# A decoder block in split float32: weight chunks brought in by a casting and an accumulating transfer in place of load, cast and subtraction

## The chip, the core and the metric

The kernel runs on one core of a Trainium2 chip. The metric is the device time of one execution in microseconds; the kernel before has a median of 1076.48 us over three runs (1075.39 to 1076.62).

## What is computed

One decoder block for 512 tokens of width 1024, all in float32, with 16 learned tokens ahead. Two branches read the same normed input: a gated delta rule (8 heads of 128, a causal convolution in front, a recurrence over chunks of tokens) and an attention that keeps the 128 keys with the highest index score for each query. The branches are gated and merged, an output product and a norm follow, then an MLP with a squared ReLU and 4096 hidden columns.

```
n = rmsnorm(h); proj = n @ w_in                      # 1024 x 8280 columns, split into q, k, v, z, gates, index parts
y_gdn = gated_delta_rule(silu(conv(q, k, v)), ...) ; y_dsa = sparse_attention(...)
merged = sigmoid(gate_a) * (y_gdn @ w_branch_gdn) + sigmoid(gate_b) * (y_dsa @ w_branch_dsa)
h = h + rmsnorm(merged @ w_out)
u = square(relu(rmsnorm(h) @ w_up)); h = h + rmsnorm(u @ w_down)
```

## The kernel before, in words

Every dense product is done in three passes so that it keeps float32's precision: both operands are split into a high part, rounded to the format `float32r` in which the tensor engine takes one pass, and a low part, the rest. A product is high x high, high x low and low x high; these three are the three matmul lines in each loop (L193 to L195, L502 to L504, L888 to L890, L1009 to L1011, L1101 to L1103).

The weights come in chunks of 128 partitions x 1024 columns, 512 KB, laid out in memory so that a row of 4 KB is contiguous. There are 152 of them and a smaller one of 704 columns (`misc`) at the start: 8 each for keys, values, queries, the delta rule's gate z, gate a, the first branch product `bg` and the second `bd`; 4 index queries; 12 in the attention (4 queries, 8 of gate b) besides 4 queries, 2 keys and 2 values ahead of it; 8 of the output product; 32 of `w_up` and 32 of `w_down`. The helper `wload` (L90) fetches one: SP issues the load into `raw` (two buffers), the scalar engine copies it with rounding into `hi` (L99), the vector engine subtracts `hi` from `raw` into `lo` (L100). `hi` and `lo` share a ring of five buffers of the tag `hl`; the chunks loaded with `spare` (the second half of the output product's and of the last down product's columns, and two chunks of the first `w_up` group) use other buffers for part of it. In most loops a chunk serves 24 products of 512 columns, for keys, values and queries 48 of 264.

The order of each engine's instructions is made at build time by a planner that takes, by priority (mostly program order), what it thinks ready at that moment by its own costs; `tc.issue_after` and `tc.high_priority` bend it in places. An engine then works through its list in order, and an instruction that waits holds up all behind it. A transfer is issued from the list of an engine: SP's list holds the weight loads, the loads of the activations `hT` (L132), of the tables and of the residual `x`, and the stores of the result. POOL's list holds small loads of constants (L83 to L87), squares of the activations (L138), memsets, the decay rows of the delta rule through memory (L267 to L275), the blocks of its matrix L and of the inverse through memory (L362 to L369, L412 to L426), a selection on `E` (L447), selections in the index scores (L774, L862), loads of norm gains (L1023, L1025, L1086) and the last multiplications (L1139).

The stages follow each other: activations and `misc` (to about 20 us), keys, values and queries with their convolutions (to about 210 us), the inverse and the recurrence with z between (to about 325 us), index scores with gates and the first branch (to about 455 us), attention with its dense products between (to about 600 us), second branch and output product (to about 700 us), and the MLP, whose up and down products alternate in four groups.

Of the kernel before, what the change touches and what calls it, by code (L numbers as in the profile page):

```python
# [10 lines left out]
F32 = mybir.dt.float32  # L11
F32R = mybir.dt.float32r
I32 = mybir.dt.int32
AF = mybir.ActivationFunctionType
ALU = mybir.AluOpType
# [4 lines left out]
P = 128  # L20
# [3 lines left out]
L = 512  # L24
T = NM + L
# [13 lines left out]
def hybrid_block(ctx: ExitStack, tc: tile.TileContext, io: dict):  # L39
# [6 lines left out]
    def f(ap):  # L46
        return ap.bitcast(F32)
# [21 lines left out]
    # ---------------------------------------------------------------- constants  # L69
# [19 lines left out]
    # ---------------------------------------------------------------- weights  # L89
    def wload(src, n, name, spare=False):  # L90
        """one chunk of weights, split; spare: in the buffers tb and st"""
        raw = wp.tile([P, 1024], F32, tag="raw", name=f"raw_{name}", bufs=2)
        nc.sync.dma_start(raw[:, :n], src)
        if spare:
            hi = wk.tile([P, 1024], F32R, tag="tb", name=f"hi_{name}", bufs=2)
            lo = cst.tile([P, 1024], F32R, tag="st", name=f"lo_{name}", bufs=2)
        else:
            hi, lo = (wp.tile([P, 1024], F32R, tag="hl", name=f"{x}_{name}", bufs=5) for x in ("hi", "lo"))
        S.copy(hi[:, :n], raw[:, :n])  # L99
        V.tensor_tensor(lo[:, :n], raw[:, :n], f(hi[:, :n]), ALU.subtract)  # L100
        return hi, lo

    def rsqrt(out, a, shape, tag):
        """out = a ** -0.5 (a > 0): Newton steps from a guess by the exponent"""
# [19 lines left out]
    # ---------------------------------------------------------------- normed activations, transposed and split  # L124
# [19 lines left out]
    def token_scales():  # L144
        """1 / rms of the tokens: on partitions (rn) and along the free axis on every partition (rb)"""
# [26 lines left out]
    # ---------------------------------------------------------------- dense products, weights stationary  # L172
    marks, todo = [], []

    def later(keep=0, part=None):
        """what the tensor engine does with earlier convolved columns, behind a part of the latest products"""
# [7 lines left out]
    def proj_a(w, name, moving=None, m=P, full=True):  # L184
        """columns of one weight chunk [P, 8, m] against the tokens: psum parts [(tile, first column, n)]"""
# [14 lines left out]
    # ---------------------------------------------------------------- small columns: index key, beta, decay, index weights  # L200
# [40 lines left out]
    # cumulated log decay in each chunk (the 16 leading tokens, then chunks of 128)  # L241
# [16 lines left out]
    # rows of gc, through memory, on every partition  # L258
# [10 lines left out]
    # decay between the tokens of a chunk: E[p, (h j), f] = exp(-|gc_p - gc_f|)  # L269
# [14 lines left out]
    # ---------------------------------------------------------------- causal convolution and silu  # L284
    silu = []

    def conv(g, c0, parts_of, out, name, wide=False):
        """out = silu(conv) of the tokens from c0"""
# [17 lines left out]
    # ---------------------------------------------------------------- keys of the delta rule  # L306
# [10 lines left out]
    # XL: blocks 0, 1 (and below them) and 2 of the inverse; XL, L1: the blocks of L below the diagonal of 64 and of 32  # L317
# [20 lines left out]
    def products(x):  # L338
        """L[c, s] = beta_c r_c^2 (k_c . k_s) E of 4 heads (i = h * 4 + j); its blocks on the diagonal, by memory, to lanes"""
# [23 lines left out]
        # lane = x * 64 + i * 4 + block  # L363
# [20 lines left out]
    # ---------------------------------------------------------------- (I + L)^-1: 32-blocks, one on each lane  # L384
# [5 lines left out]
    def substitute(nlane, n, lt, x, tmp):  # L390
        """x = (I + L)^-1 of the block of each lane, then its transpose in tmp; in steps"""
# [42 lines left out]
    # ---------------------------------------------------------------- values of the delta rule: r beta v, tokens on partitions  # L434
    vb = slots.tile([P, 32, P], F32, tag="s5", name="vb")
    vbm = cst.tile([NM, NH, P], F32, tag="st", name="vbm", bufs=2)
    for h in range(NH):
# [4 lines left out]
        if h == 1:  # L442
# [3 lines left out]
            # upper triangle (with the diagonal) of E for the scores  # L446
# [14 lines left out]
    # ---------------------------------------------------------------- queries; scores against the keys of the chunk  # L461
# [32 lines left out]
    # ---------------------------------------------------------------- dense products, tokens stationary  # L494
    def rows_part(pt, pairs, lhs, t, cs, first=True, last=True):
        """adds to one psum tile the products of some chunks [P, 2, 512], (number, (hi, lo)), for the columns cs"""
# [9 lines left out]
    def proj_half(src, name, lhs, evac):  # L506
        """512 columns for all tokens, chunk by chunk of the weights"""
# [8 lines left out]
    def proj_rows(src, name, lhs, evac, done, more=lambda t: None, tail=0):  # L516
        """all columns, so that the tiles of tokens are done one after the other: the first half, then the other tile by tile"""
# [14 lines left out]
    # ---------------------------------------------------------------- output gate of the delta rule: norm * silu(z)  # L532
# [4 lines left out]
    def z_products():  # L537
        """in pieces, for the tensor engine between the steps of others"""
# [33 lines left out]
    # ---------------------------------------------------------------- (I + L)^-1: from 32-blocks to 128  # L572
    # 32 -> 64: Y12 = -Y11 (L21^T Y22)
# [24 lines left out]
    # 64 -> 128  # L598
# [17 lines left out]
    # ---------------------------------------------------------------- the recurrence over the chunks  # L616
    def ktok(cols, n, col, h0, name):
        """keys with their decay to the end of the chunk, tokens on partitions, 4 heads"""
# [613 lines left out]
```

## Time and profile before

| | |
|---|---|
| median of three runs | 1076.48 us |
| span of the profiled execution | 1075.6 us |
| tensor engine busy | 1054.0 us, 98% |
| vector engine busy | 682.8 us, 63% |
| scalar engine busy | 461.4 us, 43% |
| POOL busy | 61.6 us, 6% |
| bytes moved by DMA | 96.44 MB, 90 GB/s in the mean |

The profiled execution's own time isn't listed apart from its span; the span lies within the three runs and 0.9 us under their median. The busy share of the tensor engine is that of matmuls that overlap in the pipeline, so it says that there are few gaps and not that each product is as fast as can be. Issuing a transfer isn't counted as busy time. A line number is that of the kernel before.

### The profile page before, as it was taken

The page shows a single profiled execution, that of the slowest core. Times are in us where ns is not written, and L with a number is a line of the kernel's source. Part 1 is how long each engine was busy: PE and PEld are TensorE (multiplying, and loading weights), DVE is VectorE, ACT ScalarE, POOL GpSimd, SP SyncE. Part 2 cuts the span into 40 slices and gives each one's busy share as a digit, 9 for nine tenths or more (in the row PEclk, how much of TensorE's full clock was granted, in tenths as well). Part 3 has the DMA queues.
Part 4 walks back from the last instruction along what each step waited for, and adds up shares of the span by engine and source line. Part 5 has one row for each costly group of instructions (what it writes and reads, how often), then busy time and mean ns, then how long its engine had stood idle before and what let it go on. Part 6 is the DMA issues. An engine that isn't in the chain of part 4 may idle for free.

```text
span 1075.6 us, 15893 instructions
## 1 busy us (share of the span) xinstructions
PE 1054.0 (98%) x6249; PEld 903.8 (84%) x6249; DVE 682.8 (63%) x1502; ACT 461.4 (43%) x854; POOL 61.6 (6%) x85
## 2 busy tenths in 40 slices
PE   6999999999999999999999999999999999999996
PEld 5999999999997678898888888898888888888885
DVE  5797899516689789957867555695442343343346
ACT  5465555444268432235665432473432332232130
POOL 4202302100000000000000000000000000000022
PEclk9999999998999999999999999999999999999999
DMA  5433424210133022232121235332322333333332
GB/s 177 117 102 108 116 82 136 68 41 2 43 101 115 20 79 80 97 99 82 56 59 59 80 90 187 96 95 83 98 88 90 97 98 98 87 90 98 98 98 79
DMA packets 28235, 96.44 MB, mean 90 GB/s; under 512 B 3632, under 2 KB 3968, under 8 KB 28160
## 3 DMA queue, kind: packets, MB, share of 16 engines
q1 hardware_dynamic: 25440, 87.51, 26.1%
q0 software_dynamic: 2720, 7.92, 2.8%
q8 instruction: 49, 0.80, 0.3%
q14 instruction: 26, 0.21, 0.1%
HBM read 90.14 MB, written 5.28 MB: 89 GB/s over the span
## 4 chain that ended last, share of the span: by engine, by line
PE 89%; DVE 6%; DMA 2%; ACT 2%; issue 1%; SPq 0%; DVEq 0%; ACTq 0%
PE up L1102 5%; PE up L1103 5%; PE up L1101 5%; PE d L503 4%; PE d L504 4%; PE d L502 4%; PE pa_dense L889 2%; PE pa_dense L890 2%; PE pa_dense L888 2%; PE pa_bg L194 1%; PE pa_q L195 1%; PE pa_q L193 1%; PE pa_q L194 1%; PE pa_bg L193 1%; PE pa_bg L195 1%; PE bd L1009 1%
## 5 line engine op out<-in xcount | busy, mean ns | idle before, releaser
L1102 PE MATMUL up<-n2l,hi_up 128*128 128x512 f32 (+1 forms) x288 | 106.8, 372 | 0.0
L1101 PE MATMUL up<-n2h,hi_up 128*128 128x512 f32 (+1 forms) x288 | 106.6, 371 | 0.0
L1103 PE MATMUL up<-n2h,lo_up 128*128 128x512 f32 (+1 forms) x288 | 106.6, 371 | 0.0
L100 DVE TENSOR_TENSOR lo_up<-raw_up,hi_up 128x1024 fp32r<-128x1024 f32 x32 | 39.2, 1225 | 71.0 <-PE up L1102 53.0
L100 DVE TENSOR_TENSOR lo_d<-raw_d,hi_d 128x1024 fp32r<-128x1024 f32 x24 | 29.4, 1226 | 78.4 <-PE d L503 56.0
L502 PE MATMUL d<-hi_d,uh 128*128 128x512 f32 x192 | 75.9, 396 | 0.0
L504 PE MATMUL d<-hi_d,ul 128*128 128x512 f32 x192 | 75.9, 395 | 0.0
L503 PE MATMUL d<-lo_d,uh 128*128 128x512 f32 x192 | 75.9, 395 | 0.0
L1102 PEld LDWEIGHTS up<-n2l,hi_up 128*128 128x128 f32 x288 | 54.2, 188 | 10.3
L1101 PEld LDWEIGHTS up<-n2h,hi_up 128*128 128x128 f32 x288 | 54.2, 188 | 10.3
L1103 PEld LDWEIGHTS up<-n2h,lo_up 128*128 128x128 f32 x288 | 54.1, 188 | 10.3
L1105 ACT ACTIVATE rup<-up 128x512 f32<-128x512 f32 (+1 forms) x36 | 19.9, 552 | 99.6 <-PE up L1103 99.6
L99 ACT CAST hi_d<-raw_d 128x1024 fp32r<-128x1024 f32 x24 | 25.2, 1049 | 59.6 <-PE d L504 59.6
L99 ACT CAST hi_up<-raw_up 128x1024 fp32r<-128x1024 f32 x32 | 33.4, 1044 | 24.0 <-PE d L504 22.7
L504 PEld LDWEIGHTS d<-hi_d,ul 128*128 128x128 f32 x192 | 36.1, 188 | 8.7
L502 PEld LDWEIGHTS d<-hi_d,uh 128*128 128x128 f32 x192 | 36.1, 188 | 8.7
L503 PEld LDWEIGHTS d<-lo_d,uh 128*128 128x128 f32 x192 | 36.1, 188 | 8.7
L888 PE MATMUL pa_dense<-nhi,hi_dense 128*128 128x512 f32 x96 | 39.3, 409 | 0.0
L889 PE MATMUL pa_dense<-nlo,hi_dense 128*128 128x512 f32 x96 | 38.0, 396 | 0.0
L890 PE MATMUL pa_dense<-nhi,lo_dense 128*128 128x512 f32 x96 | 38.0, 396 | 0.0
L546 PE MATMUL pb_z<-hi_z,nhi 128*128 128x256 f32 x128 | 37.9, 296 | 0.0
L193 PE MATMUL pa_k<-nhi,hi_k 128*128 128x264 f32 x128 | 37.1, 290 | 0.0
(570 smaller groups left out, 3079.3 us busy)
## 6 DMA issues: line engine op xcount, KB each, us to landing
raw_up<-w_up SPq DMA_DIRECT2D x32, 512.0 KB, 3.6
raw_d<-w_down SPq DMA_DIRECT2D x24, 512.0 KB, 3.6
raw_k<-w_k SPq DMA_DIRECT2D x8, 512.0 KB, 4.1
raw_v<-w_v SPq DMA_DIRECT2D x8, 512.0 KB, 4.2
raw_q<-w_q SPq DMA_DIRECT2D x8, 512.0 KB, 3.5
raw_z<-w_z SPq DMA_DIRECT2D x8, 512.0 KB, 3.6
raw_w_ga<-w_ga SPq DMA_DIRECT2D x8, 512.0 KB, 3.6
raw_bg<-w_bg SPq DMA_DIRECT2D x8, 512.0 KB, 3.6
```

The costliest lines, as they stand in the source:

```text
L99: S.copy(hi[:, :n], raw[:, :n])
L100: V.tensor_tensor(lo[:, :n], raw[:, :n], f(hi[:, :n]), ALU.subtract)
L193: TE.matmul(pt[:m, :n], hi[:, ws], mh[:, k, ms], start=(k == 0), stop=False)
L502: TE.matmul(pt, lh, whi, start=beg, stop=False)
L503: TE.matmul(pt, lh, wlo, start=False, stop=False)
L504: TE.matmul(pt, ll, whi, start=False, stop=end)
L888: TE.matmul(pt, hi[:, ws], nhi[:, k, NM:], start=(k == 0), stop=False)
L889: TE.matmul(pt, hi[:, ws], nlo[:, k, NM:], start=False, stop=False)
L890: mm = TE.matmul(pt, lo[:, ws], nhi[:, k, NM:], start=False, stop=(k == KT - 1))
L1101: TE.matmul(pt, hi[:, ws], n2h[:, k, ms], start=(k == 0), stop=False)
L1102: TE.matmul(pt, hi[:, ws], n2l[:, k, ms], start=False, stop=False)
L1103: TE.matmul(pt, lo[:, ws], n2h[:, k, ms], start=False, stop=(k == KT - 1))
```

## The change

Only `wload` changes; the other differences are removed comments. The load into `raw` goes, and with it the buffers `raw`. POOL issues a transfer from memory straight into `hi`, whose format differs from the source's, so that the transfer casts. The scalar engine then writes -`hi` into `lo`. POOL issues a second transfer of the same chunk from memory into `lo`, which adds to what stands there: `lo` becomes the source less `hi`. The subtraction on the vector engine goes. The ring `hl` has seven buffers in place of five.

```diff
     def wload(src, n, name, spare=False):
-        raw = wp.tile([P, 1024], F32, tag="raw", name=f"raw_{name}", bufs=2)
-        nc.sync.dma_start(raw[:, :n], src)
         if spare:
             hi = wk.tile([P, 1024], F32R, tag="tb", name=f"hi_{name}", bufs=2)
             lo = cst.tile([P, 1024], F32R, tag="st", name=f"lo_{name}", bufs=2)
         else:
-            hi, lo = (wp.tile([P, 1024], F32R, tag="hl", name=f"{x}_{name}", bufs=5) for x in ("hi", "lo"))
-        S.copy(hi[:, :n], raw[:, :n])
-        V.tensor_tensor(lo[:, :n], raw[:, :n], f(hi[:, :n]), ALU.subtract)
+            hi, lo = (wp.tile([P, 1024], F32R, tag="hl", name=f"{x}_{name}", bufs=7) for x in ("hi", "lo"))
+        G.dma_start(hi[:, :n], src)
+        S.activation(lo[:, :n], f(hi[:, :n]), AF.Copy, scale=-1.0)
+        G.dma_start(lo[:, :n], src, accum_op=ALU.add)
         return hi, lo
```

## Rows read from the trace of the kernel before

**Rows 1.** The page's busy time of each engine, with share and instructions.

```profile
PE 1054.0 (98%) x6249; PEld 903.8 (84%) x6249; DVE 682.8 (63%) x1502; ACT 461.4 (43%) x854; POOL 61.6 (6%) x85
```

**Rows 2.** Waits of the tensor engine: us in total, times, longest.

```profile
PE pa_misc L193 <- ACT hi_misc L99: 6.6, 1, 6.6
PE pa_misc L193 <- ACT nhi L135: 2.4, 1, 2.4
PE pa_misc L194 <- DVE nlo L136: 1.0, 1, 1.0
PE vtp L453 <- ACT cy_v L303: 0.9, 1, 0.9
```

**Rows 3.** Timeline of the scalar engine in the MLP: start, duration, instruction, idle before.

```profile
859.53 0.60 ACT L1105 ACTIVATE rup<-up 128x512 f32<-128x512 f32 x1 [3.44 <-PE up L1103]
...
865.15 0.60 ACT L1105 ACTIVATE rup<-up 128x512 f32<-128x512 f32 x1 [3.43 <-PE up L1103]
```

**Rows 4.** The page's costliest groups: a chunk's subtraction and cast; busy, mean ns.

```profile
L100 DVE TENSOR_TENSOR lo_up<-raw_up,hi_up 128x1024 fp32r<-128x1024 f32 x32 | 39.2, 1225 | 71.0 <-PE up L1102 53.0
...
L99 ACT CAST hi_up<-raw_up 128x1024 fp32r<-128x1024 f32 x32 | 33.4, 1044 | 24.0 <-PE d L504 22.7
```

**Rows 5.** Timeline of the scalar engine at the start: a scaled copy.

```profile
4.87 0.73 ACT L135 ACTIVATE nhi<-xr,gT 128x528 fp32r<-128x528 f32 x1 [2.57 <-DMA xr<-hT]
```

**Rows 6.** DMA queues (q1: SP's, q0: POOL's): packets, MB, share of 16 engines.

```profile
q1 hardware_dynamic: 25440, 87.51, 26.1%
q0 software_dynamic: 2720, 7.92, 2.8%
```

**Rows 7.** Timeline of POOL, where its dense stretches begin and end, and its waits.

```profile
2.95 0.53 POOL L87 DMA_DIRECT2D dtb<-dt_bias  x1
...
41.44 0.52 POOL L267 DMA_DIRECT2D gcd<-gts  x1 [15.59 <-DVE gts L264]
...
50.67 0.53 POOL L275 DMA_DIRECT2D zsp<-gcdm  x1
90.22 0.96 POOL L392 MEMSET sub<- 128x1024 f32 x1 [39.02 <-PE kss L333]
...
100.55 1.27 POOL L368 COPY lam<-lhs 32x512 f32<-32x512 f32 x2
...
111.35 1.16 POOL L362 DMA_DIRECT2D ld<-lhs  x1 [8.43 <-DVE lhs L360]
...
119.74 1.89 POOL L368 COPY lam<-lhs 32x512 f32<-32x512 f32 x2
...
175.17 0.53 POOL L425 DMA_DIRECT2D ym__1009<-zsp  x1 [51.61 <-DVE zsp L400]
...
191.09 0.65 POOL L417 DMA_DIRECT2D Yb<-yd  x1
...
385.55 0.29 POOL L774 TENSOR_SCALAR_AFFINE_SELECT mask<-mask 128x128 f32<-128x128 f32 x1 [16.24 <-DVE mask L772]
```

**Rows 8.** Transfers by issuing queue: count, KB each, median us from issue to landing.

```profile
raw_up<-w_up SPq DMA_DIRECT2D x32, 512.0 KB, 3.6
...
ld<-lhs POOLq DMA_DIRECT2D x2, 1024.0 KB, 7.2
...
xd<-sub POOLq DMA_DIRECT2D x1, 512.0 KB, 5.2
```

**Rows 9.** The chain that ended last, in the keys: start, duration, piece.

```profile
57.28 1.11 PE kss L333 x10
64.32 1.11 PE kss L333 x10
```

**Rows 10.** Timeline of the tensor engine at the start.

```profile
7.32 0.42 PE L194 MATMUL pa_misc<-nlo,hi_misc 128*88 128x264 f32 x1
7.54 0.47 PE L195 MATMUL pa_misc<-nhi,lo_misc 128*88 128x264 f32 x1
...
19.81 0.28 PE L193 MATMUL pa_k<-nhi,hi_k 128*128 128x264 f32 x1
```

**Rows 11.** A window of the MLP: busy us by engine, granted clock, DMA share, GB/s.

```profile
800.00:900.00 100.00, 100.00 (x430) 80.45 (x429) 33.19 (x35) 32.22 (x43) 0.00 (x0) 1.00 0.31 95
```

## Prediction

> **What bounds the kernel now.** I read the page's busy shares first, then who waits for whom on the tensor engine, then one chunk of the MLP as a timeline, then the DMA views, and last the timeline of POOL, the queue into which the change moves the weights.
>
> The tensor engine is busy for 98% of the span, the vector engine for 63%, the scalar engine for 43%, POOL for 6% [rows 1]. What the tensor engine waited for is 10 us at the start, for the first weights and activations (6.6, 2.4 and 1.0), and later one wait of 0.9 us [rows 2]; the five left out have 0.2 to 0.8 us each. It never waited for a weight chunk behind the first. In the MLP a chunk of 512 KB gives 24 products of 512 columns; the activation behind one follows the one before after 5.62 us (859.53, 865.15) [rows 3], and the tensor engine fills that time. So the weights need only be in place in time, and they are. An engine that is relieved off this path gives back at most what the tensor engine waits for it: some 3 us.
>
> The span is 1075.6 us; the three runs have a median of 1076.48, so I work from the span and add 0.9.
>
> **What goes.** 152 chunks (and one small one) lose a subtraction on the vector engine, 1.23 us each [rows 4], together 187 us of its 683. Almost all of it lies beside products. Of the stalls that it may have a part in, 0.9 us before a transpose and 1.0 us at the start [rows 2] among them, I count -2 us (bounds 0 and -3). SP loses its 152 loads; it keeps the activations and tables, and nothing waits for SP.
>
> **What stays in size.** The scalar engine's cast of a chunk (1.04 us [rows 4]) becomes a scaled copy of the same 1024 columns. The nearest row for a scaled copy is 0.73 us for 528 columns [rows 5], so at most 1.4 us for 1024; once in 5.62 us that changes nothing.
>
> **What is added: two transfers in series on POOL's queue.** Neither a casting nor an accumulating transfer stands in the trace, so I bound them by plain rows.
>
> First the rate. SP's queue moved 87.51 MB in 26.1% of 16 engines' span [rows 6]: 87.51 / (16 x 0.261 x 1075.6 us) is 19.5 GB/s for each engine, so 512 KB take 1.68 us of all 16. POOL's queue moved 7.92 MB in 2.8%, 16.4 GB/s, or 2.0 us for 512 KB, with smaller packets among them. For the cast I take 1.68 to 2.0 us. The accumulation must read memory and the buffer, twice the reading: 3.4 to 4.0 us if reading sets the pace. The pair then needs 5.0 to 6.0 us of the DMA engines in each 5.62 us. That is the narrowest place of this change: at 5.0 it is hidden, at 6.0 each chunk comes 0.4 us late.
>
> No row shows an accumulation, so here a page speaks. The Trainium skill, "Collectives: The Full Stack", section "The bandwidth ceiling: the fold count and why AG ≠ RS ≠ AR", says that a reduction in the DMA path is slow because it reads two sources, not because it adds, and gives 31 GB/s over two engines for it. By that, as an estimate, 16 engines would take 2.1 us for 512 KB, the pair about 4 us, and the MLP's term below would fall to 0. I keep the rows' own 5.0 to 6.0.
>
> Second the latency. With 7 buffers taken in turn, the low part of chunk i gets the buffer of the high part of chunk i-3, and the high part of chunk i that of the low part of chunk i-4. So the low part may be begun when chunk i-3 ends and is wanted when chunk i-1 ends: two chunks, 11.2 us in the MLP. In it lie the activation that is ahead on the scalar engine and the scaled copy (0.6 [rows 3] and 1.05 to 1.4), the issue on POOL (0.5 to 1.2 us [rows 7]) and the landing. For the landing the nearest rows are 3.6 us for a chunk from SP's queue, 5.2 us for 512 KB from POOL's, and 7.2 us for 1 MB from POOL's, which moves as much as an accumulation reads [rows 8]; I take 6 to 7.2. The chain is 8 to 10 us; with the next high part in front on the same queue (1.7 to 2.0 us) it is 10 to 12. If the chain is 12, three chunks take 12 + 5.62, that is 5.87 for each instead of 5.62.
>
> So rate and latency both sit at the edge, between 0 and 0.4 us for each chunk. Chunks at this pace: 64 of the MLP, 8 of the second branch product, 16 of the first gates and branch, 88 in all. 88 x 0.4 is 35 us at most; I take 0.16 each, **+14 us**, nearer the hidden end, because a plain load of 4 KB rows is the nearer row for both rates.
>
> **What POOL's order adds.** POOL works through its queue in order, so a load stands behind whatever waits there: the low part's accumulation itself waits for the scalar engine, and behind it the next high part, memsets, copies and stores of the delta rule. Before, POOL's waits hurt nobody. Four stretches are dense [rows 7]: 41.4 to 51.2 us (decay rows, eight broadcasts), 90.2 to 101.8 (a store, a read that waits for it, copies), 111.4 to 121.6 (the same and a selection), 175.2 to 191.7 (blocks of the inverse): 9.8, 11.6, 10.2 and 16.6 us. A chunk of the keys lasts 7.0 us [rows 9], so the chain of 8 to 10 us leaves 4 to 6 us of two chunks to spare. If loads stood wholly behind each stretch, the losses beyond 5 us would be 4.8 + 6.6 + 5.2 + 11.6 = 28 us. If the planner sets loads between these instructions, they are near 0. I take a third, **+10 us**. Later POOL waits for the vector engine's index scores four times, for instance 16.2 us before the selection at 385.6 [rows 7]. A load behind it would lose up to 11 us, one ahead of it nothing; these loads are free early, and I take **+2 us**.
>
> **The start.** The first weights now go behind POOL's three small loads, whose last begins at 2.95 us [rows 7]; the first product waited 6.6 us [rows 2], the first with a low part began at 7.54 us [rows 10]. Now: issue at 3.5, landing 3.6 to 7.2 later, copy 0.8, issue 0.7, landing 5.2 to 7.2 again: low part at 14 to 19 us. Before, the stage waited 2.4 and 1.0 us for activations anyway [rows 2], and the next stage's first product came at 19.81 us [rows 10]. 32 of the 48 products need no low part and can run meanwhile; the other 16 begin 0.22 us apart, as 7.32 and 7.54 [rows 10]. Done at 18 to 23 us instead of 19.8; the next chunk's low part queues behind. Bounds -1 and +8, taken **+4 us**.
>
> **Sum.** 1075.6 + 14 + 10 + 2 + 4 - 2 = 1103.6; with the 0.9, **1104.5 us**. The forecast's own range is 1085 to 1130.
>
> **Rivals.**
> *The DMA engines become the bound.* If an accumulation doesn't overlap with its neighbours, or the cast slows its transfer too, the pair exceeds 5.62 us, and from there each further microsecond costs 88. With 6.6 us it is 86 us on top of the other 14 (POOL, the start, less DVE): 1176 us. With 7.2 us, one landing time of 1 MB, it is 139: 1230. For it speaks that POOL's queue was the slower one per byte [rows 6]; against it that plain rows already give 5.0. Chance 0.25, from 1130 to 1230.
>
> *All of it is hidden, not slower.* The DMA pair stays at 5.0 us, the planner sets the loads ahead of POOL's waits, and the start hides behind the activations' own waits (2.4 and 1.0 us [rows 2]). It decides where the chain stays under two chunks everywhere. Then the change is -3 to +2 us: 1073 to 1078.6. Against it: four dense stretches and the series of two landings at the start. Chance 0.16.
>
> *A load behind a long wait on POOL.* POOL waited 51.6 us for the substitution before the store at 175.17, and up to 16.2 us later [rows 7]. If the planner takes that vector work for earlier than it is, loads stand behind it: about 45 us beyond the spare time, on top of the 28: 1150 us. Chance 0.08.
>
> *POOL can't write its transfers while the vector engine works.* In the trace the same pair of copies on POOL took 1.27 us at 100.55 and 1.89 us at 119.74 [rows 7], so POOL is slowed by something there. If each issue grew by 0.7 us, a chain with two would be 1.4 us longer and a chunk 0.47 us: 88 x 0.47 = 41 more, 1146 us. The Trainium skill, "SBUF — State Buffer", section "Who interferes with whom", says that a vector instruction in a two-port mode holds the port pair that POOL needs for descriptors. By that rule it would come so only beside copies and scalar operations, of which the MLP has few. Chance 0.04.
>
> That the transfer doesn't round, both formats having 4 bytes, would leave a low part of zero and the same time: no case of its own.
>
> **How the numbers follow.** Forecast 0.47, then 0.25, 0.16, 0.08, 0.04. A measurement of this kernel can tell about 0.2%, 2.15 us, from no change. Below 1074.3 lies 0.06 (part of the hidden case), between 1074.3 and 1078.6 0.10, above 0.84. The range 1075 to 1200 leaves out about 0.08 below and 0.10 above, the DMA bound at its worst.
>
> **What would show it.** SP's queue should fall from 87.5 MB to about 8, POOL's rise to some 160, and the DMA share in the MLP from 0.31 [rows 11] to about 0.9. The vector engine should lose some 187 us. New waits of the tensor engine should name transfers into low parts: short ones spread over the MLP (rate or latency), and blocks of several microseconds near 45, 95, 115 and 185 us (POOL's order). If the activations of the MLP still follow each other after 5.62 us, the 14 us are wrong; if after 6.5, the DMA bound holds. No wait at all, or waits on the scalar engine's negatives instead of transfers, would make the reasoning wrong.

## The result, and the profile after

The changed kernel takes 1135.22 us in the median (1130.21 to 1143.03, 4 runs) beside 1076.55 for the kernel before: 1.0548 times as long, 95% interval 1.0505 to 1.0591. I had forecast 1104.5, so the side was right and the rise forecast was half of the measured one. Runs of one kernel differ with the granted clock: these four from 1130.21 us at a mean clock of 0.978 to 1143.03 at 0.966, and those of before, over all chips, from 1075.4 to 1092.8. The profiled execution has a span of 1134.9 us, 59.3 more than the 1075.6 of before. Lines of code below are the changed kernel's: L97 the casting transfer, L98 the negative, L99 the accumulating transfer.

The page's busy times (answers [rows 1]), its two DMA queues ([rows 6]), the negative of an up chunk (mean 1061 ns, [rows 4]), the transfers of these chunks with their median landing ([rows 8]), and, in a fence of its own, the window of the MLP ([rows 11]):

```profile
PE 1072.5 (95%) x6249; PEld 918.4 (81%) x6249; DVE 518.4 (46%) x1349; ACT 463.4 (41%) x854; POOL 278.1 (25%) x391
...
q0 software_dynamic: 46784, 168.04, 68.9%
q1 hardware_dynamic: 3408, 7.44, 1.9%
...
L98 ACT ACTIVATE lo_up<-hi_up 128x1024 fp32r<-128x1024 f32 x32 | 34.0, 1061 | 75.2 <-DMA hi_up<-w_up 35.5
...
hi_up<-w_up POOLq DMA_DIRECT2D x32, 512.0 KB, 5.2
lo_up<-w_up POOLq DMA_DIRECT2D x32, 512.0 KB, 7.5
```

```profile
800.00:900.00 100.00, 100.00 (x429) 80.39 (x428) 15.93 (x23) 36.09 (x48) 26.35 (x37) 1.00 0.92 196
```

The change does what it says: the vector engine loses 164 us, the weights have moved to POOL's queue twice over, and in the MLP the DMA engines' share rises from 0.31 to 0.92. And there the tensor engine is busy for all of the 100 us at full clock, as before. POOL's 278.1 us contain its issues, contrary to what is said of issues beside the table of before: the page counts the 32 of the up chunks' high parts as 18.4 us. The time was lost elsewhere. The tensor engine's waits (us in total, times, longest; answers [rows 2]):

```profile
PE pa_misc L192 <- DMA hi_misc<-w_misc: 12.4, 1, 12.4
PE pa_misc L194 <- DMA lo_misc<-w_misc: 7.9, 1, 7.9
PE pa_v L194 <- DMA lo_v<-w_v: 5.7, 2, 4.5
PE is L765 <- DVE iq L745: 4.9, 1, 4.9
PE pb_z L546 <- DMA lo_z<-w_z: 4.9, 2, 3.6
PE kss L332 <- ACT cy_k L325: 3.3, 1, 3.3
PE up L1102 <- DMA lo_up<-w_up: 3.0, 1, 3.0
PE pa_q L194 <- DMA lo_q<-w_q: 2.9, 1, 2.9
PE oa L502 <- DMA lo_oa<-w_out: 2.6, 1, 2.6
PE pa_k L194 <- DMA lo_k<-w_k: 2.3, 1, 2.3
PE bd L1010 <- DMA lo_bd<-w_bd: 2.0, 1, 2.0
```

Eight of the eleven lines name a low part, that is the second transfer of a chunk. All waits of this view come to 53.7 us, those of before to 12.7: 41 of the 59.3. The rest is about what the granted clock costs. The windows of 10 us around the waits of the keys (3.3 and 2.3) show it; the columns are busy us of PE, PEld, DVE, ACT and POOL, the granted clock, the DMA share and GB/s:

```profile
55.00:65.00 10.00, 6.66 (x57) 6.43 (x56) 7.99 (x17) 4.77 (x11) 1.58 (x2) 1.00 0.52 153
65.00:75.00 10.00, 7.56 (x33) 6.95 (x33) 5.29 (x9) 4.43 (x10) 2.50 (x4) 0.50 1.05 222
75.00:85.00 10.00, 10.00 (x84) 9.68 (x83) 3.01 (x4) 5.07 (x10) 1.93 (x3) 0.99 0.74 147
```

From 65 to 75 us the clock is at 0.50, its lower level of 1.2 GHz, and then full again. The stretch begins 1.2 us behind the stall of 3.3 us; the one of 2.3 us lies in it. The record of the granted clock has eight such stretches between the start and the tail, of 3.4 to 10.2 us, 51.0 together; in before it has one (6.8 us, in the recurrence). Six of the eight, 34.0 us, begin in a stall of 2.0 to 4.9 us or at most 1.2 us behind it; 6 us of them lie inside stalls, and half of the other 28 is 14 us. The two others (10.2 us in the recurrence, 6.8 in the index scores) follow no wait and cost 8.5, before's one 3.4. That makes 19 us, beside 18 that the waits leave over.

Where the tensor engine falls behind is read from the first product of each stage, in us later than in before. The other columns are experiments that follow:

| stage begins | after | x4 | x9 | x10 | x17 | x16 | x1 |
|---|---|---|---|---|---|---|---|
| keys | 11.0 | 8.9 | -1.9 | 5.3 | 8.7 | -1.0 | 6.6 |
| values | 19.9 | 16.4 | 0.0 | 3.7 | 14.9 | -0.9 | 4.8 |
| queries | 26.2 | 16.9 | 7.6 | 1.6 | 22.1 | -1.1 | 9.5 |
| z, recurrence | 29.6 | 18.1 | 11.0 | 3.0 | 22.2 | -1.1 | 17.3 |
| index scores | 37.8 | 30.3 | 16.2 | 3.9 | 24.8 | -1.1 | 20.7 |
| attention | 47.5 | 50.8 | 25.8 | 23.0 | 40.1 | -1.1 | 20.8 |
| second branch | 48.4 | 51.3 | 26.7 | 23.6 | 40.6 | -1.3 | 20.4 |
| output product | 52.3 | 52.5 | 28.8 | 23.6 | 40.7 | -1.2 | 20.5 |
| up products | 55.9 | 54.8 | 33.6 | 24.4 | 41.5 | -0.4 | 20.5 |
| down products | 59.3 | 58.7 | 37.2 | 24.1 | 46.0 | 7.4 | 21.8 |
| last product | 59.3 | 58.7 | 37.2 | 24.1 | 46.0 | 7.4 | 21.8 |

After loses 30 us up to z, 8 in z and the recurrence, 10 in the index scores, 12 from the attention to the first chunks of the MLP, and nothing behind them.

Two places show how a stall comes about. At the start (timeline of the tensor engine, answers [rows 10]):

```profile
12.39 0.49 PE L192 MATMUL pa_misc<-nhi,hi_misc 128*88 128x264 f32 x1 [12.39 <-DMA hi_misc<-w_misc]
...
21.47 0.52 PE L194 MATMUL pa_misc<-nhi,lo_misc 128*88 128x264 f32 x1 [7.92 <-DMA lo_misc<-w_misc]
```

The first transfer was issued at 3.52 us beside the eight loads of the activations and landed 8.7 us later; its negative stood behind squares in the scalar engine's list until 15.69; the second transfer was issued at 16.77 and landed at 21.4. In the values, the timelines of the scalar engine and of POOL around the wait of 4.5 us:

```profile
132.73 1.06 ACT L98 ACTIVATE lo_v<-hi_v 128x1024 fp32r<-128x1024 f32 x1 [1.65 <-DMA hi_v<-w_v]
```

```profile
130.90 3.97 POOL L446 TENSOR_SCALAR_AFFINE_SELECT E<-E 128x4096 f32<-128x4096 f32 x1
136.50 1.11 POOL L363 DMA_DIRECT2D lam<-ld  x1 [1.63 <-DMA ld<-lhs]
137.65 1.47 POOL L367 COPY lam<-lhs 32x512 f32<-32x512 f32 x2
139.18 1.04 POOL L368 COPY lam<-lhs 64x1024 f32<-64x1024 f32 x1
140.17 0.94 POOL L99 DMA_DIRECT2D lo_v<-w_v  x1
```

The negative is there at 133.8, but the accumulation is issued only at 140.17, behind a selection, a read that waits for a store, and copies. Something else stands beside the selection: of 24 steps of the vector engine on `cy_v`, 0.76 us in the median, the one begun at 131.21 took 4.2 us.

### The profile page after: what moved, and what is told of

It is laid out like the page before. It is cut to its first block, busy times and chain, and to the rows that moved or that the text cites. A ratio compares the mean times of both kernels' runs of the same rounds, so it can differ in the third digit from the quotient of the medians.

```text
span 1134.9 us, 15954 instructions
## 1 busy us (share of the span) xinstructions
PE 1072.5 (95%) x6249; PEld 918.4 (81%) x6249; DVE 518.4 (46%) x1349; ACT 463.4 (41%) x854; POOL 278.1 (25%) x391
## 3 DMA queue, kind: packets, MB, share of 16 engines
q0 software_dynamic: 46784, 168.04, 68.9%
## 4 chain that ended last, share of the span: by engine, by line
PE 68%; issue 11%; DMA 8%; DVE 8%; ACT 3%; POOL 2%; SPq 0%; DVEq 0%; POOLq 0%; ACTq 0%
PE up L1102 5%; PE up L1101 5%; PE up L1100 5%; PE d L503 4%; PE d L502 4%; PE d L501 4%; PE pa_dense L887 2%; PE pa_dense L888 2%; PE pa_dense L889 2%; DVE cy_v L300 2%; PE pa_w_ga L192 1%; PE pa_w_ga L193 1%; PE pa_w_ga L194 1%; PE pa_bg L192 1%; PE pa_bg L193 1%
## 5 line engine op out<-in xcount | busy, mean ns | idle before, releaser
L1106 DVE TENSOR_TENSOR uup<-rup 128x512 f32<-128x512 f32 (+1 forms) x36 | 22.7, 632 | 144.5 <-ACT rup L1104 144.5
L98 ACT ACTIVATE lo_up<-hi_up 128x1024 fp32r<-128x1024 f32 x32 | 34.0, 1061 | 75.2 <-DMA hi_up<-w_up 35.5
L1100 PEld LDWEIGHTS up<-n2h,hi_up 128*128 128x128 f32 x288 | 54.7, 190 | 10.2
L1101 PEld LDWEIGHTS up<-n2l,hi_up 128*128 128x128 f32 x288 | 54.6, 189 | 10.2
L98 ACT ACTIVATE lo_d<-hi_d 128x1024 fp32r<-128x1024 f32 x24 | 25.4, 1060 | 83.2 <-DMA hi_d<-w_down 57.2
L97 POOL DMA_DIRECT2D hi_up<-w_up x32 | 18.4, 574 | 114.7 <-PE up L1102 62.2
L194 PE MATMUL pa_v<-nhi,lo_v 128*128 128x264 f32 x128 | 37.4, 294 | 5.7 <-DMA lo_v<-w_v 5.7
L546 PE MATMUL pb_z<-lo_z,nhi 128*128 128x256 f32 x128 | 37.6, 294 | 4.9 <-DMA lo_z<-w_z 4.9
L194 PE MATMUL pa_k<-nhi,lo_k 128*128 128x264 f32 x128 | 37.8, 299 | 2.3 <-DMA lo_k<-w_k 2.3
L194 PE MATMUL pa_q<-nhi,lo_q 128*128 128x264 f32 x128 | 36.4, 285 | 2.9 <-DMA lo_q<-w_q 2.9
```

What stands on the lines that cost most here:

```text
L98: S.activation(lo[:, :n], f(hi[:, :n]), AF.Copy, scale=-1.0)
L194: mark = TE.matmul(pt[:m, :n], lo[:, ws], mh[:, k, ms], start=False, stop=(k == KT - 1))
L546: TE.matmul(pt, nhi[:, k, ts], wlo, start=False, stop=False)
L1100: TE.matmul(pt, hi[:, ws], n2h[:, k, ms], start=(k == 0), stop=False)
L1101: TE.matmul(pt, hi[:, ws], n2l[:, k, ms], start=False, stop=False)
L1106: V.tensor_tensor(u, r, r, ALU.mult)
```

## The experiments

Theories at the outset: **Q**, the order: loads stand behind what waits in POOL's list, negatives behind the scalar engine's. **T**, the transfers: two for each chunk, one after the other, each slower than a plain one and colliding with others on the 16 engines. Later **C**: a stall lowers the clock, so it costs more than its length; **C2**: in the index scores the order of the products alone lowers it. Ratios are to the runs of the kernel before on the same chip.

### One part at a time: x1, x2, x3

All three start from the kernel before, with its two raw buffers and its ring of five. x1 (shown): the raw loads from POOL. x2: the high part by the casting transfer from POOL, the low part still by SP's raw load and the subtraction. x3: the low part by negative and accumulation.

```diff
-        nc.sync.dma_start(raw[:, :n], src)
+        nc.gpsimd.dma_start(raw[:, :n], src)
```

> The kernel before, with its plain weight loads issued from POOL's list instead of SP's; cast and subtraction stay. Theory Q (order: the loads stand behind POOL's other work and the scalar engine's): the single transfer needs no second issue, but it waits in the same list, so a good part of the 59 us should appear, 1095 to 1120 us. Theory T (transfers: two in series, and slower ones): one plain transfer per chunk, so nearly no loss, 1076 to 1085 us.

> The high part by the casting transfer from POOL; the low part as before, a plain load by SP and the subtraction on the vector engine; the bytes moved double. Theory Q: the high parts wait in POOL's list, 1090 to 1115 us. Theory T: the casting transfer alone is about a plain one and nothing follows it in series but a subtraction, 1076 to 1090 us.

> The high part as before (plain load by SP, cast on the scalar engine); the low part by the negative and the accumulating transfer from POOL. Theory Q: the accumulation still waits in POOL's list and behind the scalar engine's negative, 1095 to 1120 us. Theory T: the series of two transfers stays, only the first is a faster one (3.6 us to land instead of 5.2), and the start's series too: 1100 to 1125 us. If the accumulation were harmless, under 1085 us.

x1: 1103.39 us, ratio 1.0245 (1.0220 to 1.0271). x2: 1114.96, 1.0356 (1.0302 to 1.0411). x3: 1276.6 (1256 to 1289), without a ratio. x1 and x2 lie in theory Q's ranges, x2 at their upper end, x3 beyond those of both. POOL's queue with two raw buffers thus costs 27 us, nearly what I had forecast for the whole change, with plain transfers and one for each chunk: at the start (6.6) and from the values to the index scores (4.8 to 20.7, table). x2 has two transfers for each chunk, neither behind the other, and loses 38 us, 24.7 of them up to the index scores; its longest wait behind the start, 5.3 us, is for a high part. So a series isn't needed for a loss; the few buffers of x1 and x2 are a cause that no run tries by itself. x3 is worse than the whole change, with waits for low parts all over the MLP:

```profile
PE d L504 <- DMA lo_d<-w_down: 25.7, 14, 2.7
PE up L1104 <- DMA lo_up<-w_up: 15.0, 16, 2.4
```

It keeps the ring of five, in which a low part takes the buffer of the high part two chunks back; with the change's seven it is three chunks back. I take that chunk of time for what lets the MLP of after hide its accumulations; no run varies the ring by itself.

### The transfers by themselves: x5

Twelve chunks of 512 KB for each way, the decoder block left out.

> The disputed cost by itself; the whole block is left out. Five phases, each behind the one before: 12 plain chunk loads from SP, 12 plain from POOL, 12 casting, 12 accumulating, then 6 casting and 6 accumulating in turns, each of 512 KB, back to back. Theory T: the accumulation is the slow one, 3.4 to 4.5 us each against 1.6 to 2.0 for the others, and a pair in turns takes 5 us or more. Theory Q: all four kinds stream alike, under 2.2 us each, a pair under 4.4 us.

The page's row of GB/s, 40 slices of 4.86 us: plain from SP (305 to 417), plain from POOL (356 to 419), casting (343 to 417), accumulating (205 to 213), and pairs of casting and accumulating (224 to 290):

```profile
GB/s 0 0 0 305 409 417 165 0 0 55 356 419 414 69 343 417 414 104 0 0 34 208 205 211 212 208 213 4 0 0 146 224 267 290 284 84 0 0 187 246
```

A row of 4 KB takes a DMA engine 159 ns plain from either queue, 174 casting, 328 accumulating: 1.27, 1.39 and 2.62 us for 512 KB (8 rows on each of the 16 engines). A pair takes 4.0 us by that sum, within the 5.62 us of a chunk in the MLP. Casting is almost free, and the accumulation takes 2.06 times a plain load.

### What the accumulation costs in place: x10, x17

```diff
-        G.dma_start(lo[:, :n], src, accum_op=ALU.add)      (x10: gone)
+        G.dma_start(lo[:, :n], src)                        (x17: overwrites the negative)
```

> The changed kernel without the accumulating transfer: the low part is left at the high part's negative, so the low products are computed with other values. What stays is the casting transfer from POOL, the scalar engine's negative and seven buffers. Theory T: the second transfer carries more than half of the 59 us, 1085 to 1105 us. Theory Q: it is the lists' order, which stays, 1110 to 1130 us.

> After, with the second transfer of each chunk as a plain casting one that overwrites the negative: the low part is then the rounded weights themselves and not the remainder. The order of all instructions, the buffers, the waits and the number of transfers stay; only a row of 4 KB takes 174 ns of a DMA engine instead of 328, as measured alone. If what the accumulation costs is its time on the DMA engines (collisions with tables, activations and the delta rule's transfers): most of the 33 us by which after is behind the kernel without the second transfer comes back: 1100 to 1115. If it is the second transfer in series, begun behind the scalar engine's negative and POOL's list, with its landing of some 4 to 5 us instead of 7.5: 1118 to 1135.

x10: 1101.68, ratio 1.0214 (1.0164 to 1.0265). x17: 1125.56, 1.0420 (1.0350 to 1.0489). The whole change is at 1.0548, so of its 59 us some 23 stay without a second transfer, 22 come with a second transfer of any kind, and 14 with its adding. Without it, POOL's lists and the first transfers cost 3.9 us up to the index scores (table; 1.6 to 5.3 on the way), beside 24.8 in x17 and 37.8 in after. 19 of the 23 fall in the index scores at half clock, which comes and goes between runs (below; x10's four went from 1092 to 1105), so the split is better read ahead of that stage: 4, 21 and 13 us. The tensor engine's waits of x10, and then of x17:

```profile
PE pa_misc L191 <- DMA hi_misc<-w_misc: 12.5, 1, 12.5
PE pa_misc L193 <- ACT lo_misc L98: 2.6, 1, 2.6
PE pk L650 <- ACT osb L667: 1.0, 1, 1.0
```

```profile
PE pa_v L194 <- DMA lo_v<-w_v: 6.2, 2, 3.2
PE pa_misc L194 <- DMA lo_misc<-w_misc: 6.0, 1, 6.0
PE up L1102 <- DMA lo_up<-w_up: 4.2, 1, 4.2
```

Low parts are late in x17 as in after, though each row takes 174 ns and not 328; those of the queries, the second branch and the output product no longer are. So most of the cost is that of a second transfer, whatever it does. I put it down to the series: the second can be issued only when the first has landed and the negative is made. No run has a second transfer outside the series with these buffers, so its traffic isn't told apart from its place.

### Whose list: x4, x8, x9

x4: after, with POOL's 21 other transfers moved to SP. x8: after, the negative on the vector engine. x9: after, with the first four chunks (`misc`, three keys) the old way.

```diff
-        S.activation(lo[:, :n], f(hi[:, :n]), AF.Copy, scale=-1.0)
+        V.tensor_scalar(lo[:, :n], f(hi[:, :n]), -1.0, None, ALU.mult)      (x8)
```

> The changed kernel, with all 21 places of POOL's other transfers (constants, decay rows, blocks of L and of the inverse, gains) issued from SP's list, which the change has emptied; POOL keeps memsets, copies, selections and the weights. Theory Q: the blocks near 45, 130 and 185 us go, 1105 to 1120 us, and the stalls that stay are at the start and where the scalar engine's list is late. Theory T: nothing moves, 1130 to 1140 us, because the same transfers still share the 16 engines.

> After, with the negative made by the vector engine in place of the scalar engine: nothing else changes, both transfers stay. Theory Q in its second form (the accumulation waits for its negative, which stands behind squares, copies and exponentials in the scalar engine's list): the low parts of the first chunks, of the keys and of the values come some microseconds earlier and 1110 to 1125 is to be expected. Theory T (the second transfer itself, begun after the first has landed): the negative only changes its list, the vector engine has long lists of its own in keys, values and index scores, and the time stays at 1128 to 1145.

> The changed kernel, with the first four chunks (misc and three of the keys) brought in the old way: plain load by SP, cast, subtraction. If the start's 11 us come from the series of two transfers, the keys begin at about 20 us and the whole ends 10 to 18 us earlier, 1117 to 1126 us. If later waits only move, the end stays at 1130 to 1137.

x4: 1132.0, ratio 1.0486 (1.0439 to 1.0533). It gains 10 us in the values and queries (table: 16.9 and 18.1 instead of 26.2 and 29.6), so the case at 140.17 us is real, and loses them again in the recurrence and the index scores, where 30.7 us ran at half clock. As a whole it lies in theory T's range, and its interval overlaps after's. x8: 1149.78, 1.0645 (1.0585 to 1.0706), slower than either theory said: its waits for lo_v reach 10.6 and for lo_q 8.6 us. By the index scores it is 7 us behind after (45.0 and 37.8); the rest of the 17 us between the two traces comes in that stage, with 34.1 us at half clock. x9: 1121.26, 1.0430 (1.0384 to 1.0477), in the range expected: the start is gone (-1.9 at the keys), the rest stays.

### What a stall costs: x6, x11

x6 repeats the subtraction of three chunks. x11 makes the fourth chunk of groups 1 to 3 wait for the activation of the third (shortened: `x` is the chunk's high part with `n` 1, 4 and 12, and its low part with 1; the two chunks behind it get one pass for each part):

```diff
+    for _ in range(n):
+        V.scalar_tensor_tensor(x[:, :512], r_of_third_chunk, 0.0, f(x[:, :512]), ALU.mult, ALU.add)
```

> The kernel before with three stalls made on purpose in the MLP, 100 us and more apart: the subtraction of one chunk is repeated, 5, 8 and 12 times in all (4.9, 8.6 and 13.5 us later), of which the chunk's spare time hides some 4.4 us. If a stall costs what it lasts, the stalls of about 0.5, 4 and 9 us make 13.5 us: 1090 us. If each also leaves the tensor engine at the low clock for a stretch, as in the changed kernel's record of the clock (3.4 to 10.2 us at 0.5), each of the two long ones costs 2 to 5 us more: 1094 to 1100 us.

> The kernel before, with the loads as they were. In the up products of groups 1, 2 and 3 the weights of the fourth chunk are made to wait for the activation of the third: 1, 4 and 12 passes of the vector engine (0.69 us each for 512 columns, as the squares in the MLP of before take) add zero times that activation to the high part, one more to the low part (the fifth and sixth chunk get one pass for each part, which fit beside products). So the tensor engine must stand three times: about 0.6 us for the activation, 0 to 0.7 for the square that may stand ahead, and 0.69 for each pass: 1.5 to 2.7 us, 4 to 5, and 9.5 to 10.5, together 15 to 18 us. No transfer is added. If a stall of the tensor engine itself brings the half clock (theory C, the term missing from the sum), the two long stalls, and perhaps the short one, are each followed within some microseconds by a stretch at half of the granted clock of 3.4 to 10 us, which costs half of its length again: 1095 to 1103 us, the mean clock of the MLP under 1. If the low clock of after comes from the transfers' traffic or from something else in its early stages, the clock stays full in the MLP and the time is 1091.5 to 1094.5.

x6: 1080.37, ratio 1.0029 (1.0018 to 1.0041). The delays were hidden; the longest stall was 1.2 us and no half clock followed it, so it told nothing of theory C. x11: 1105.18, ratio 1.0252 (1.0215 to 1.0288). The three stalls came out at 2.38, 6.6 and 12.41 us, 21.4 together, and the kernel takes 28.7 us more in the profiled execution. The windows behind each (granted clock is the third number from the end):

```profile
772.00:775.00 3.00, 2.81 (x8) 2.12 (x9) 2.45 (x5) 0.09 (x1) 0.00 (x0) 0.64 0.56 175
...
870.00:875.00 5.00, 4.61 (x11) 3.68 (x12) 0.25 (x1) 0.00 (x0) 0.00 (x0) 0.50 0.00 0
876.00:881.00 5.00, 5.00 (x23) 4.04 (x22) 2.76 (x4) 2.16 (x3) 0.00 (x0) 1.00 0.16 15
...
967.00:981.00 14.00, 6.02 (x14) 4.79 (x15) 7.56 (x12) 0.00 (x0) 0.00 (x0) 0.51 0.00 0
981.00:990.00 9.00, 9.00 (x40) 7.19 (x39) 4.64 (x6) 2.88 (x5) 0.00 (x0) 1.00 0.22 58
```

In 5 us at half clock 11 products run, and 23 in the next 5 us. The half clock lasted from 772.8 to 776.2, 868.4 to 875.2 and 967.4 to 981.0. Product by product against before, the three places cost 4.2, 9.0 and 15.4 us. Less the stalls that is 1.8, 2.4 and 3.0, half of the part of each stretch that lies behind its stall (3.4, 4.8 and 6.0 us). So a stall alone, with the old loads, brings the half clock here, and theory C holds. It is no rule for every stall: in after those of 2.9 us in the queries and 2.6 in the output product were followed by none. The Trainium skill, "TensorE: Matmul & The Clock Gate", section "Terms", prices throttled time in the same way: time that runs at half of the clock costs half of its length; this trace agrees.

### Where the MLP stands: x12, x16

The new way for the 64 chunks of the MLP alone. In x12 the others came the old way with all their chunks in the ring of seven; in x16 they keep the buffers of before.

> After's way for the 64 chunks of the MLP alone; the other 89 come by SP's plain load, the scalar engine's cast and the vector engine's subtraction, their raw chunks in the same ring of seven. If the MLP hides the pair of transfers (in after nothing was lost there behind its first chunks, at a DMA share of 0.9 and more): 1076 to 1080, and only the four chunks that start the MLP together may cost something (in after 3.0 us of waits and a stretch at half clock, so at most 6 us: 1083), with the granted clock as in before. If the MLP of after was hidden only because something ahead of it was late, or if the DMA bound of my prediction holds: 1085 and above, the up and down products late by 0.1 us and more for each chunk.

> The new way for the 64 chunks of the MLP alone, as before tried, but now the 89 other chunks keep their two raw buffers and the ring of five, and the MLP's chunks go through these seven in turn. So the stages ahead are those of the kernel before, product by product. If the MLP hides the pair of transfers: 1076 to 1082, with at most the 3.6 us that the last trial lost behind the first four chunks of the up product. If the DMA bound of my prediction holds in the MLP (a pair over 5.62 us): 1130 and more; if the pair is at the edge, as my sum had it (0.16 for each of 64 chunks): 1086.

x12: 1113.76, ratio 1.0313 (1.0257 to 1.0370), but 32 us of that are lost ahead of the MLP, where I had also changed the ring for the old loads; how much is the ring's no run shows. x16: 1085.08, 1.0056 (1.0012 to 1.0101). It is level with before up to the MLP, loses all of it at the first four up chunks, which are begun together, and nothing in the 60 behind (table: 7.4 and 7.4). Its waits:

```profile
PE up L1116 <- DMA hi_up<-w_up: 3.7, 1, 3.7
PE up L1118 <- DMA lo_up<-w_up: 2.5, 2, 1.9
```

The two long ones (3.7 and 1.9 us) and half of the 5.5 us at half clock behind them are the whole loss. The time is near the 1086 of the expectation for a pair at the edge, but by accident: that loss would be spread over 64 chunks. The MLP hides the pair wherever the loads are ahead.

### The index scores: x13, x14b, x15

x10 loses 19 us in this stage with no wait over 1 us in it. Its windows:

```profile
370.00:380.00 10.00, 10.00 (x22) 5.29 (x22) 7.01 (x19) 4.26 (x10) 0.28 (x1) 0.63 0.20 53
380.00:390.00 10.00, 10.00 (x22) 6.16 (x22) 3.49 (x8) 2.10 (x6) 0.00 (x0) 0.50 0.00 0
390.00:400.00 10.00, 10.00 (x22) 5.81 (x21) 2.09 (x5) 1.65 (x5) 0.00 (x0) 0.50 0.00 0
```

The stage has 80 score products (L764 and L765) among dense ones. When loads are late in the planner's reckoning, it sets the dense products elsewhere: in after 16 score products stand in a row, in before at most 10. x13 has this stage's chunks the old way; x14b is the kernel before with one dense chunk asked for earlier, so that 14 stand in a row; x15 is after with at most 8.

```diff
-    "... s1 a0 b0 s2 s3 a1 a2 b1 ..."
+    "... s1 a0 b0 a1 s2 s3 a2 b1 ..."      (x14b, the old loads)
+    "... s1 s2 a0 b0 s3 a1 a2 b1 ..."      (x15, the new loads)
```

> After, but the 20 chunks of the index queries, gate a and the first branch (the index-score stage) come by plain load, cast and subtraction. That stage took 9.6 us more in after, with a wait of 4.9 us for the rotated index queries beside a late table and a low clock behind it. If the stage's own transfers did that (theory T): the stage end is later than its beginning by 0 to 2 us only, and the time 1121 to 1129. If what matters is the state in which the stage begins (late z chunks, the low clock from ahead, theory C) the stage stays some 8 to 10 us longer and the time within 1130 to 1143.

> The kernel before, its loads as they were; only in the index-score stage the second chunk of gate a is asked for ahead of the third and fourth index scores instead of behind them. By the build order 14 score products of the tensor engine then stand in a row where before had at most 10, behind a block of dense products. In the kernels with transfers so far, a half-clock stretch began at the end of such a row of 12 to 16 (after: row at 404.5 to 410.3 us, half clock from 409.7; the kernel without the accumulation: 368.7 to 375.3, from 372.7), and none in the kernels with at most 10 and the old loads. If the order of the products brings the low clock (theory C2), a stretch at half clock begins at the end of that row and the stage takes 3 to 18 us more than 141.5: 1080 to 1095. If it is the transfers' traffic or the late weights there, the clock stays full and the time is 1074 to 1079.

> After, with the third index score asked for ahead of the first gate and branch chunk: by the build order no more than 8 score products stand in a row (16 in after). Theory C2: the half-clock stretch that began at the end of the 16 (409.7 us, 6.8 us long; 30 to 37 us in some variants) is gone, the one behind the stall of 4.9 us stays, the stage takes 145 to 149 us instead of 151.2: 1125 to 1132. If the order of these products has no part in it: stage within 150 to 160, time within 1130 to 1143.

x13: 1128.06, ratio 1.0461 (1.0416 to 1.0506), within what theory T expected. Its trace is of its longest execution (1144.1 us; the other three 1127 to 1129), so it isn't set against after's; in it the stage took 157.5 us with 37.6 at half clock, without the stage's own transfers and with at most 10 score products in a row, as in before. x14b: 1082.44 (1079.69 to 1090.73). In its profiled execution the row of 14 stood from 364.9 to 370.0 us and the clock was at half from 369.3 for 34 us, without any wait, and the stage took 155.9 us instead of 141.5:

```profile
370.00:380.00 10.00, 10.00 (x22) 6.05 (x22) 5.02 (x13) 2.68 (x6) 0.29 (x1) 0.50 0.00 0
380.00:390.00 10.00, 10.00 (x23) 5.76 (x21) 1.95 (x4) 2.34 (x6) 0.00 (x0) 0.50 0.00 0
```

So the low clock there needs none of the new transfers. But the ratio, 1.0036 (0.9996 to 1.0077), doesn't separate this kernel from before: its trace is of its longest run, and before's own on that chip went up to 1090.9 us, at a mean clock of 0.977 where x14b's traced run has 0.978 and most of before's have 0.994. Where in before that clock was lost no trace shows. So one trace is no proof of C2, and x13 speaks against it. x15: 1135.63, 1.0526 (1.0451 to 1.0602), stage 155.1 us, half clock for 13.7 us from 374.4, around a stall of 4.7 us, and for 10.2 from 422.2. The expected gain isn't there; the time and the stage are those expected if the order had no part in it. What holds the clock down in this stage stays open.

## Why the prediction was wrong

The step that failed is the price of a late low part ahead of the MLP. The sum charged the series of two landings at the start (+4) and as a small rate in the steady loops, and trusted elsewhere to the 4 to 6 us that the chain leaves to spare; measured are 11 us at the start, 19 instead of +10 from the keys to z, and 8 in z and the recurrence, which had no term. And a stall was priced at its length: the clock behind it was put at nothing, and 41 us of waits became 59.

It was right in its side, in what bounds the kernel, in the counts (SP's queue falls to 7.4 MB, POOL's rises to 168, the MLP's DMA share 0.92 against the 0.9 I named; the vector engine's busy time fell by 164 us and not by 187), and in expecting transfers into low parts as the new waits. The range held the time only because the DMA bound had widened it; the forecast's own range, up to 1130, did not. Term by term:

- **The MLP and its like, +14.** The 0.16 us for each chunk was wrong: it is 0, or several us in one place. My bounds from plain rows ([rows 6]) said 5.0 to 6.0 us for a pair. Alone it takes 4.0 (x5); in place POOL's queue moved 168.04 MB in 68.9% of 16 engines' time, 2.44 us for 512 KB and 4.9 for a pair. So the lower bound held, and it was the hidden one. The chain held too: 0.6, 1.06 and 0.87 us and a landing of 7.5 are 10. What does cost is where several pairs begin together or beside another large transfer: 3.9 us in the second branch, 2.8 in the output product, 3.4 at the first up chunks (x16: 7.8 there). That these 10 us are near my 14 is luck.
- **The start, +4 with 8 as the bound.** It is 11. I took the first landing for 3.6 to 7.2 us and it was 8.7, beside the activations' loads; I left out that the negative stands behind the scalar engine's squares. By the medians of x9 and after the start is worth 14 us at the end, with runs of each that spread over 13.
- **POOL's order, +10.** From the keys to the beginning of z it is 19. I had the cause only in part. Of the four dense stretches that I named (two of them go on for one copy more than I read, to 102.9 and 123.1 us), stalls stand behind the first (3.3 and 2.3 us), the third (4.5) and the fourth (2.9), and the 3.3 us, a wait for `cy_k`, are 4.6 in x4, so they aren't POOL's. x4 takes POOL's other transfers away and gains 10 from the keys to z; x10 leaves them and takes the second transfer away, and all but 3 to 4 us are gone. It is not POOL's list as such but the second transfer, which I take to have no time left in its series (landing, negative, POOL, landing again) where anything else is late. x1 loses more than x10 on the same list with one transfer for each chunk; it has only two raw buffers behind it, to which I put that down without a run.
- **Index-score waits, +2.** It is 10 in that stage, and 8 in z and the recurrence ahead of it, for which I had no term (z's low parts 4.9 in the waits above). The stage's one long wait, 4.9 us, is for the vector engine's `iq`; none of the waits on POOL that I named shows.
- **The vector engine's relief, -2.** Nothing of it is seen. The 164 us lay beside products, as argued.
- **What the sum lacked.** No term for the clock. Some 14 us of it came with stalls, and x11 shows that with the old loads; 5 came without a wait ahead and stay open. Nor for the planner: other loads give another order of the tensor engine's products, even where no load is late; what that costs no run shows.

Of the rivals, the DMA bound (0.25, from 1130 to 1230) has the time in its range by accident: no chunk behind the first is late in the MLP. The Trainium skill, "Collectives: The Full Stack", section "The bandwidth ceiling: the fold count and why AG ≠ RS ≠ AR", which says that a reduction reads two sources, was the better guide for a pair by itself: by it I had estimated 2.1 us for an accumulation, a pair of 4 and an MLP term of 0; measured alone are 2.62 (and 2.06 times a plain row, for which it says two readings) and 4.0, in place 4.9, and the term is 0. The load behind a long wait on POOL (0.08, 1150): the accumulation at 140.17 us is such a one, of 6 us and not 45. POOL hindered by the vector engine (0.04): an issue takes 0.55 to 0.70 us casting and 0.85 to 0.88 accumulating in the medians of the stages, and 0.53 and 0.86 in x5 where the vector engine is idle; so no growth of 0.7 us was there. The rule of the Trainium skill, "SBUF — State Buffer", section "Who interferes with whom", that the rival drew on, a vector instruction in a two-port mode that holds POOL up, is shown by no run here. What the traces show is a vector engine held up beside POOL: the step of 4.2 us at the selection, where before has a subtraction of 3.5 us instead of 1.2. Hidden throughout (0.16) is refuted.

## What to carry to other kernels

Ask of a load not only whether its rate fits, but how many landings stand one behind the other from the moment a buffer is free, and look for the stages where other transfers or full lists leave no slack: there each chunk costs, and in the steady loop none does. Price a stall of the tensor engine above its length, since it may go on at half clock afterwards. Before a stage's time in one trace is put down to an edit, look whether the mean clock is the same from run to run: that of the kernel before itself went from 0.994 down to 0.977.

## What the runs showed of the hardware

- In full slices a casting transfer ran at 414 to 417 GB/s, a plain one at 409 to 419, an accumulating one at 205 to 213 (x5). Alone the two new ones take 1.39 and 2.62 us for 512 KB; in the MLP they land 5.2 and 7.5 us after their issue.
- Stalls of the tensor engine of 2.38, 6.6 and 12.41 us were each followed by, or ran into, a stretch at 1.2 GHz (3.4, 6.8 and 13.7 us), in a loop that otherwise stayed at 2.4 GHz up to the tail (x11). Stalls of 2.9 and 2.6 us in after were not.
- The clock also stood at half for 34 us in a stage without a single wait over 1 us (x10, and x14b with the old loads), where score products stand among dense ones.
- A step of the vector engine beside POOL's selection of 4.0 us took 4.2 us instead of 0.76 (after), a subtraction 3.5 instead of 1.2 (before).
